# A 2-layer hybrid decoder trunk on one core: weight splits of 128x2048 in one instruction per engine

## The chip, the cores and the metric

One Trainium2 chip, one core. The time is the device time of one execution in microseconds (us), as the median of the runs of a kernel. The engines are TensorE (PE), VectorE (DVE), ScalarE (ACT), GpSimd (POOL) and SyncE (SP); each works through its own queue of instructions in order. TensorE's weight loads are shown apart, as PEld.

## What is computed

256 tokens of 1024 channels pass through two layers in float32. Each layer runs three mixers side by side, merges them with sigmoid gates, projects, and then applies a feed-forward part, which is dense in layer 0 and routed over 8 experts in layer 1.

```python
for l in range(DEPTH):                                   # 2 layers
    z = rms_norm(x, norm_mix_g[l]) @ w_in[l]
    a_x, a_y, m_u, m_o, m_i, m_f, xa_q, gate_pre = split_columns(z)
    xa_c = causal_dwconv(a_x, conv_rg_w[l], conv_rg_b[l])          # 4 taps
    y_rg = rg_lru(xa_c, rg_w_a[l], ..., rg_w_x[l], ...) * gelu(a_y)  # block-diagonal w_a, w_x, then a scan
    y_ml = mlstm_branch(m_u, m_o, m_i, m_f, ...)                   # conv, silu, block-diagonal w_q, w_k, w_v
    y_xa = memory_attention(xa_q, rms_norm(mem, mem_norm_g[l]), w_kv[l])   # 4 heads, softmax over 256 tokens
    x = x + (g0 * (y_rg @ w_br_rg[l]) + g1 * (y_ml @ w_br_ml[l]) + g2 * (y_xa @ w_br_xa[l])) @ w_out[l]
    h2 = rms_norm(x, norm_ffn_g[l])
    x = x + (swiglu(h2, w1, w3, w2) if l == 0 else moe_swiglu(h2, ...))   # 8 experts, 2 per token, inner size 3584
return rms_norm(x, final_norm_g)
```

## The kernel before

Every matmul keeps float32 accuracy by splitting both operands into a rounded part and a remainder. A weight raw becomes whi, a copy rounded to fp32r by ACT (line 115), and wlo = raw - whi, which DVE writes (line 116); both lines are the helper `split`. PE then makes three passes: whi with the rounded activations, whi with their remainder, wlo with the rounded ones (`passes`, line 103).

Weights come from memory as half slabs of 128x2048 (8 KB per partition) into tiles named raw (or rawu, in the expert stage), loaded by SP. `wsplit` splits each half slab in two pieces of 128x1024, each into a pair (whi, wlo) of tiles from a pool with PARTS = 5 buffers for each of the two names. A buffer is free again when PE has read the split that is in it, so a new split can start when the fifth one before it is used up. Where each piece is read depends on the stage:

- `ws_half` and `ws_slab`: weights are stationary, 256 tokens stream. A half slab feeds 48 matmuls of 256 columns. The slabs of the input projections, of the merges and of the output projection (lin.0, lin.1, ...) go this way.
- `wm_slab`: activations are stationary and 512 weight columns stream. linm.0 to linm.3 in layer 0 (linm.8 to linm.11 in layer 1) make the mLSTM's o gate this way, as two slabs; o (line 575) is the sigmoid of a finished bank, mm.
- `rglru` (the recurrence) and `mlstm`: five block-diagonal weights (w_a, w_x, w_q, w_k, w_v), one half slab each, with four blocks or heads. Two blocks were split at a time.
- The dense feed-forward part (`second` in `ffn`) and the expert stage: `wm` for w1 and w3, `second` for w2. In the expert stage there are 8 experts with 7 chunks of 512 inner columns, 56 chunks in all. A chunk reads six half slabs: two of r1, two of r3, two of w2. silu (line 876) needs the whole r1 result, the mul (line 879) needs r3, then PE transposes the product (con,t) and ACT and DVE split it (gh, gl), to be used with the w2 of the chunk in the following one.

Around the places that the change touches: in the attention each head has kT,q matmuls, a row maximum (line 260), exp (line 266), a normalisation (line 270), four transposes (ax<-con,t), a copy of the transposed tile (line 276) and the t,v matmuls; the o gate's matmuls of linm are placed among the heads. In the recurrence the output of lin.8 to lin.11 (mm) is copied by ACT (line 250), scaled by line 285 and gathered by DVE with three taps a block (line 288, conv); gh and gl are the split of the conv's result, which the block-diagonal matmuls read.

The order of instructions on an engine isn't written out in the kernel. The framework takes the program, its dependencies and the buffer pools, and orders each engine's queue; a change of sizes or of buffer numbers moves instructions in all queues.

## Time and profile before

| what | value |
|---|---|
| median of 3 runs | 2062.35 us (2060.28 to 2065.11) |
| profiled execution | 2060.13 us, span 2058.2 us |
| PE, PEld, DVE, ACT, POOL busy | 98%, 87%, 76%, 66%, 0% |
| mean granted TensorE clock | 0.994 |
| splits, raw and rawu | 772 and 228 of 128x1024 |

The stages follow one another: layer 0 until about 630 us, layer 1's mixers from there, the router from 1033 us, the experts from 1049 us to the end. An engine that is busy 98% of the span still has gaps, and what ended each one is read in the timeline, where a row's bracket gives the idle time before it and the instruction that ended it.

### The profile page before, as it was taken

How to read it: one execution, taken by the hardware profiler on the slowest of the kernel's cores; microseconds unless marked ns; L12 is line 12 of the kernel's file. 1: busy time of each engine (PE TensorE's matmuls, PEld its weight loads, DVE VectorE, ACT ScalarE, POOL GpSimd, SP SyncE). 2: the span in 40 equal slices, each digit the busy share in tenths (PEclk: the TensorE clock that was granted, in tenths of full speed). 3: DMA queues.
4: the chain of work that ended last, by engine and by line, in shares of the span. 5: the costliest groups of instructions: out<-in, count | busy, mean ns of one | idle time of the engine just before them, and what ended most of it. 6: DMA issues, size and time to landing. Idle time of an engine off the chain costs nothing.

```text
span 2058.2 us, 31849 instructions
## 1 busy us (share of the span) xinstructions
PE 2014.7 (98%) x12782; PEld 1797.8 (87%) x12782; DVE 1564.9 (76%) x1872; ACT 1352.5 (66%) x1684; POOL 3.9 (0%) x8
## 2 busy tenths in 40 slices
PE   8999999999999999999989999999999999999998
PEld 7989999999999989999968888888787787878886
DVE  8465976665555665965579999988888888888887
ACT  5575954554445566954477877777676777767775
POOL 0000000000000000000000000000000000000000
PEclk9999999999999999999999999999999999999999
DMA  8523365545555523455758898999889998999993
GB/s 328 185 83 123 144 246 193 192 172 201 187 202 186 183 105 103 164 210 205 279 223 320 339 354 352 367 356 350 342 341 350 356 364 342 339 349 353 351 365 128
DMA packets 74315, 531.82 MB, mean 258 GB/s; under 512 B 8624, under 2 KB 8752, under 8 KB 10032
## 3 DMA queue, kind: packets, MB, share of 16 engines
q1 hardware_dynamic: 73296, 528.56, 68.7%
q8 instruction: 102, 1.67, 0.3%
q10 hardware_dynamic: 864, 1.15, 0.2%
q14 instruction: 53, 0.43, 0.1%
HBM read 528.63 MB, written 1.05 MB: 257 GB/s over the span
## 4 chain that ended last, share of the span: by engine, by line
PE 92%; ACT 3%; DVE 3%; issue 1%; DMA 0%; SPq 0%; ACTq 0%; DVEq 0%
PE mm L103 65%; PE ax L103 25%; DVE wlo L116 1%; PE mm L107 1%; ACT whi L115 1%; DVE xc L288 1%; PE ax L107 1%; ACT cv L285 0%; DMA mem<-memT 0%; ACT t L266 0%; ACT u L815 0%; ACT cv L414 0%; DVE y L859 0%; ACT gh L115 0%; ACT L266 0%
## 5 line engine op out<-in xcount | busy, mean ns | idle before, releaser
L116 DVE TENSOR_TENSOR wlo<-raw,whi 128x1024 fp32r<-128x1024 f32 x772 | 925.9, 1221 | 319.9 <-ACT whi L115 313.4
L115 ACT ACTIVATE whi<-raw 128x1024 fp32r<-128x1024 f32 x772 | 800.0, 1059 | 384.9 <-PE mm L103 319.2
L103 PE MATMUL mm<-nh,wlo 128*128 128x256 f32 x1344 | 372.1, 277 | 1.9 <-DVE wlo L116 1.9
L103 PE MATMUL mm<-nh,whi 128*128 128x256 f32 x1344 | 372.2, 277 | 0.0
L103 PE MATMUL mm<-nl,whi 128*128 128x256 f32 x1344 | 371.4, 276 | 0.0
L103 PE MATMUL mm<-wlo,Xh 128*128 128x512 f32 x896 | 354.7, 396 | 4.0 <-DVE wlo L116 3.9
L103 PE MATMUL mm<-whi,Xh 128*128 128x512 f32 x896 | 352.8, 394 | 2.5 <-DVE Xl L775 2.1
L103 PE MATMUL mm<-whi,Xl 128*128 128x512 f32 x896 | 350.0, 391 | 0.0
L116 DVE TENSOR_TENSOR wlo<-rawu,whi 128x1024 fp32r<-128x1024 f32 x228 | 273.4, 1220 | 16.0 <-ACT whi L115 13.3
L103 PEld LDWEIGHTS mm<-nh,wlo 128*128 128x128 f32 x1344 | 252.4, 188 | 2.3 <-DVE wlo L116 2.2
L103 PEld LDWEIGHTS mm<-nl,whi 128*128 128x128 f32 x1344 | 252.4, 188 | 0.1
L103 PEld LDWEIGHTS mm<-nh,whi 128*128 128x128 f32 x1344 | 252.4, 188 | 0.1
L115 ACT ACTIVATE whi<-rawu 128x1024 fp32r<-128x1024 f32 x228 | 230.8, 1054 | 17.1 <-PE mm L103 6.1
L103 PEld LDWEIGHTS mm<-wlo,Xh 128*128 128x128 f32 x896 | 168.3, 188 | 54.6 <-DVE wlo L116 22.1
L103 PEld LDWEIGHTS mm<-whi,Xh 128*128 128x128 f32 x896 | 168.3, 188 | 40.5 <-DVE Xl L775 2.9
L103 PEld LDWEIGHTS mm<-whi,Xl 128*128 128x128 f32 x896 | 168.3, 188 | 33.3
L103 PE MATMUL ax<-wlo,gh 128*128 128x512 f32 (+1 forms) x496 | 191.1, 385 | 0.0
L103 PE MATMUL ax<-whi,gl 128*128 128x512 f32 (+1 forms) x496 | 188.5, 381 | 0.0
L103 PE MATMUL ax<-whi,gh 128*128 128x512 f32 (+1 forms) x496 | 171.9, 379 | 0.0
L103 PEld LDWEIGHTS ax<-whi,gh 128*128 128x128 f32 x496 | 93.1, 188 | 18.2
L103 PEld LDWEIGHTS ax<-wlo,gh 128*128 128x128 f32 x496 | 93.2, 188 | 17.0
L103 PEld LDWEIGHTS ax<-whi,gl 128*128 128x128 f32 x496 | 93.1, 188 | 16.3
(330 smaller groups left out, 2833.2 us busy)
## 6 DMA issues: line engine op xcount, KB each, us to landing
raw<-e SPq DMA_DIRECT2D x222, 1024.0 KB, 6.3
rawu<-e SPq DMA_DIRECT2D x114, 1024.0 KB, 8.3
raw<-lin SPq DMA_DIRECT2D x96, 1024.0 KB, 4.8
raw<-f SPq DMA_DIRECT2D x42, 1024.0 KB, 4.8
raw<-linm SPq DMA_DIRECT2D x16, 1024.0 KB, 4.8
raw<-bdw SPq DMA_DIRECT2D x10, 1024.0 KB, 4.8
mem<-memT SPq DMA_DIRECT2D x4, 512.0 KB, 6.3
x<-xT SPq DMA_DIRECT2D x1, 1024.0 KB, 12.4
```

The source lines that it names most:

```text
L103: nc.tensor.matmul(o, lhsT, rhs, start=start, stop=stop, **kw)
L107: nc.tensor.transpose(o, i, con[0:n, C_ID:C_ID + n])
L115: act(hi, src, AF.Copy)
L116: dve.tensor_sub(lo, src, hi.bitcast(F32))
L288: stt(dst[:, b, s:], src[:, b, :T - s], lcol(l, wo + 8 * k, b), dst[:, b, s:], op0=OP.mult, op1=OP.add)
```

## The change

A half slab is split by one instruction on ACT and one on DVE, and PE's loops read it in the same order of channels as before. The pool has three pairs of 128x2048 instead of five of 128x1024. The block-diagonal weights are split whole, before their loop over heads; the gate weights' pair (gh, gl in line 556) uses the same larger tiles. The scratch memory of the DMA goes from 2048 to 1024.

```diff
-PARTS = 5
+PARTS = 3
...
-    def half(shape, tag, at):
-        return view(wp.tile([P, 1024 + PAD], F32R, tag=tag, name=nm(tag), bufs=PARTS), shape, at)
-
-    def wsplit(src, at):
-        shape = list(src.shape)
-        hi, lo = half(shape, "whi", at[0]), half(shape, "wlo", at[1])
-        split(hi, lo, src)
+    def part(shape, tag, at):
+        return view(wp.tile([P, 2048 + PAD], F32R, tag=tag, name=nm(tag), bufs=PARTS), shape, at)
+
+    def wsplit(raw, at):
+        shape = list(raw.shape)
+        hi, lo = part(shape, "whi", at[0]), part(shape, "wlo", at[1])
+        split(hi, lo, raw)
         return hi, lo
...
     def ws_half(raw, xh, xl, ps):
+        wh, wl = wsplit(raw, WS_AT)
         for h in range(2):
-            wh, wl = wsplit(raw[:, h * 4:(h + 1) * 4], WS_AT)
...
     def wm_slab(src, xh, xl, done):
...
-        for q in range(4):
-            wh, wl = wsplit(raw[q // 2][:, (q % 2) * 2:(q % 2 + 1) * 2], WM_AT)
-            for t in range(2):
-                for k in range(2):
-                    kk = q * 2 + k
+        for q in range(2):
+            wh, wl = wsplit(raw[q], WM_AT)
+            for t in range(2):
+                for k in range(4):
+                    kk = q * 4 + k
...
         raws = (bd_load(0, l), bd_load(1, l))
+        ws_ = [wsplit(w, WS_AT) for w in raws]
         for gg in range(0, 4, 2):
-            ws_ = [wsplit(w[:, gg:gg + 2], WS_AT) for w in raws]
...
+        wv = wsplit(raw, WS_AT)
         for gg in range(0, 4, 2):
-            wv = wsplit(raw[:, gg:gg + 2], WS_AT)
...
         def wm(raw, xh, xl, cs, ps):
-            for q in range(4):
-                wh, wl = wsplit(raw[q // 2][:, (q % 2) * 2:(q % 2 + 1) * 2], WM_AT)
-                for k in range(2):
-                    kk = q * 2 + k
+            for q in range(2):
+                wh, wl = wsplit(raw[q], WM_AT)
+                for k in range(4):
+                    kk = q * 4 + k
...
-    nc = bacc.Bacc("TRN2", target_bir_lowering=False, num_devices=1, dynamic_dma_scratch_size=2048)
+    nc = bacc.Bacc("TRN2", target_bir_lowering=False, num_devices=1, dynamic_dma_scratch_size=1024)
```

The functions `second` of both feed-forward parts and the w_q and w_k loop of `mlstm` are changed in the same way. In what follows a number after a name tells tiles of one name apart; lines of the changed kernel after 620 stand two to four further down than before.

First, ACT at the end of layer 0's attention, before. The exp of head 3 is the second row; mm184 and mm185 are the two banks of the o gate that linm.2 and linm.3 fill:

```order
L266 ACT_TABLE_LOAD
L266 ACTIVATE t2163_1202,asm164_1203<-ax160_1193,anb162_1200 128x256 x2
L414 ACT_TABLE_LOAD
L414 ACTIVATE cv215_1431<-cv215_1431 128x512 x2
L276 ACTIVATE t2167_1215<-ax166_1210 128x512
L115 ACTIVATE whi221_1475<-raw219_1471 128x1024
L414 ACTIVATE cv215_1431<-cv215_1431 128x512
L115 ACTIVATE whi223_1479<-raw220_1473 128x1024
L115 ACTIVATE xah131_1098<-ax168_1217 128x512
L575 ACT_TABLE_LOAD
L575 ACTIVATE o169_1224<-mm184_1301 128x512
L575 ACTIVATE o169_1224<-mm185_1302 128x512
```

The same place in the changed kernel, where these two banks are mm148 and mm149, exp of head 3 is the L266 row with ax128, and whi205 is the split of w_v:

```order
L575 ACT_TABLE_LOAD
L575 ACTIVATE o137_1160<-mm148_1229 128x512
L115 ACTIVATE gh_186_1404<-cv175_1351 128x512
L575 ACTIVATE o137_1160<-mm149_1230 128x512
L115 ACTIVATE gh_190_1442<-cv175_1351 128x512
L266 ACT_TABLE_LOAD
L266 ACTIVATE t2131_1138,asm132_1139<-ax128_1129,anb130_1136 128x256 x2
L115 ACTIVATE whi205_1562<-raw204_1560 128x2048
L276 ACTIVATE t2135_1151<-ax134_1146 128x512
L115 ACTIVATE xah99_1034<-ax136_1153 128x512
```

The exp has moved from ahead of both o copies to behind them, and the split of w_v stands between it and the copy of the transposed tile (L276). On PE the last rows of linm.3, the transposes of head 3 and its t,v matmuls now follow each other:

```order
L103 MATMUL mm149_1230<-whi152_1259,nh23_258 128x512
L103 MATMUL mm149_1230<-wlo153_1260,nh23_258 128x512
L103 MATMUL mm149_1230<-whi152_1259,nl24_259 128x512
L107 MATMUL ax134_1146<-con_74,t2131_1138 128x128 x4
L103 MATMUL ax136_1153<-t2135_1151,v9_122 128x256 x4
```

The last matmul of linm.3 and the transposes that read t2131, which is normalised from that exp, are neighbours; before, five rows of linm.3 stood behind the transposes and seven behind t,v.

Second, DVE at the start of layer 0's recurrence, before. xc is the conv's result, gl_345 and gl_349 are those of blocks 0 and 1, and the L288 rows come in sixes, one six for each bank that lin.8 to lin.11 fill:

```order
L116 TENSOR_TENSOR wlo341_2238<-raw338_2233,whi340_2237 128x1024
L116 TENSOR_TENSOR wlo343_2242<-raw339_2235,whi342_2241 128x1024
L116 TENSOR_TENSOR gl_345_2246<-xc335_2198,gh_344_2245 128x512
L288 SCALAR_TENSOR_TENSOR xc335_2198<-ax304_1932,vec_73,xc335_2198 128x255 x2
L288 SCALAR_TENSOR_TENSOR xc335_2198<-ax304_1932,vec_73,xc335_2198 128x254 x2
L288 SCALAR_TENSOR_TENSOR xc335_2198<-ax304_1932,vec_73,xc335_2198 128x253 x2
L116 TENSOR_TENSOR gl_349_2281<-xc335_2198,gh_348_2280 128x512
L116 TENSOR_TENSOR wlo353_2316<-raw338_2233,whi352_2315 128x1024
L116 TENSOR_TENSOR wlo355_2320<-raw339_2235,whi354_2319 128x1024
L288 SCALAR_TENSOR_TENSOR xc335_2198<-ax304_1932,vec_73,xc335_2198 128x255 x2
```

The same in the changed kernel, where they are gl_291 and gl_295 and the last three L288 rows belong to lin.11's bank, mm272:

```order
L288 SCALAR_TENSOR_TENSOR xc281_2090<-ax258_1840,vec_73,xc281_2090 128x253 x2
L116 TENSOR_TENSOR wlo289_2134<-raw285_2127,whi288_2133 128x2048
L288 SCALAR_TENSOR_TENSOR xc281_2090<-ax258_1840,vec_73,xc281_2090 128x255 x2
L288 SCALAR_TENSOR_TENSOR xc281_2090<-ax258_1840,vec_73,xc281_2090 128x254 x2
L288 SCALAR_TENSOR_TENSOR xc281_2090<-ax258_1840,vec_73,xc281_2090 128x253 x2
L116 TENSOR_TENSOR gl_291_2138<-xc281_2090,gh_290_2137 128x512
L116 TENSOR_TENSOR gl_295_2173<-xc281_2090,gh_294_2172 128x512
L116 TENSOR_TENSOR wlo312_2304<-raw308_2298,whi311_2303 128x2048
```

And ACT there, in the changed kernel (whi311 is the split of lin.12):

```order
L115 ACTIVATE gh_290_2137<-xc281_2090 128x512
L115 ACTIVATE gh_294_2172<-xc281_2090 128x512
L115 ACTIVATE whi311_2303<-raw308_2298 128x2048
L250 ACTIVATE ax258_1840<-mm272_2011 128x512
L285 ACTIVATE xc281_2090<-ax258_1840,vec_73 128x256 x2
```

Both gl have moved behind the last six conv steps, and these need L250's copy of mm272, which stands behind whi311. Before, gl_345 and gl_349 stood ahead of them.

Third, ACT in a late chunk of the experts, before: raw2718 and rawu2719 are r1, raw2720 and raw2721 are r3.

```order
L115 ACTIVATE gh_2716_16543<-mm2715_16538 128x512
L115 ACTIVATE whi2723_16556<-raw2718_16547 128x1024
L115 ACTIVATE whi2725_16566<-raw2718_16547 128x1024
L115 ACTIVATE whi2727_16576<-rawu2719_16549 128x1024
L115 ACTIVATE whi2729_16586<-rawu2719_16549 128x1024
L115 ACTIVATE whi2733_16599<-raw2720_16551 128x1024
L115 ACTIVATE whi2735_16609<-raw2720_16551 128x1024
L876 ACTIVATE t22731_16596<-mm2722_16555 128x512
L115 ACTIVATE whi2737_16619<-raw2721_16553 128x1024
L115 ACTIVATE whi2739_16629<-raw2721_16553 128x1024
L115 ACTIVATE whi2743_16644<-rawu2741_16640 128x1024
```

In the changed kernel, where raw1998 and rawu1999 are r1, raw2000 and raw2001 are r3:

```order
L115 ACTIVATE whi2003_15116<-raw1998_15107 128x2048
L115 ACTIVATE gh_1996_15103<-mm1995_15098 128x512
L115 ACTIVATE whi2005_15132<-rawu1999_15109 128x2048
L115 ACTIVATE whi2009_15151<-raw2000_15111 128x2048
L115 ACTIVATE whi2011_15167<-raw2001_15113 128x2048
L880 ACTIVATE t22007_15148<-mm2002_15115 128x512
L115 ACTIVATE whi2015_15188<-rawu2013_15184 128x2048
L115 ACTIVATE whi2017_15204<-raw2014_15186 128x2048
L115 ACTIVATE whi2027_15238<-raw2022_15229 128x2048
L115 ACTIVATE gh_2020_15225<-mm2019_15220 128x512
```

silu (L876, now L880) has moved from between the two half slabs of r3 to behind both.

## Rows read from the trace of the kernel before

**Rows 1.** The page's busy times: us, share of the span, instructions.
```profile
PE 2014.7 (98%) x12782; PEld 1797.8 (87%) x12782; DVE 1564.9 (76%) x1872; ACT 1352.5 (66%) x1684; POOL 3.9 (0%) x8
```
**Rows 2.** The page's chain that ended last, by engine.
```profile
PE 92%; ACT 3%; DVE 3%; issue 1%; DMA 0%; SPq 0%; ACTq 0%; DVEq 0%
```
**Rows 3.** The page's groups: count | busy us, mean ns | idle before, releaser.
```profile
L116 DVE TENSOR_TENSOR wlo<-raw,whi 128x1024 fp32r<-128x1024 f32 x772 | 925.9, 1221 | 319.9 <-ACT whi L115 313.4
L115 ACT ACTIVATE whi<-raw 128x1024 fp32r<-128x1024 f32 x772 | 800.0, 1059 | 384.9 <-PE mm L103 319.2
```
**Rows 4.** Timeline, late expert chunks, ACT and DVE: start, us, [idle before <-releaser].
```profile
1454.33 2.00 ACT L115 ACTIVATE whi<-raw 128x1024 fp32r<-128x1024 f32 x2
...
1470.99 0.60 ACT L876 ACTIVATE t<-mm 128x512 f32<-128x512 f32 x1 [2.89 <-PE mm L103]
...
1488.12 0.60 ACT L876 ACTIVATE t<-mm 128x512 f32<-128x512 f32 x1 [2.91 <-PE mm L103]
...
1455.41 2.36 DVE L116 TENSOR_TENSOR wlo<-raw,whi 128x1024 fp32r<-128x1024 f32 x2 [1.32 <-ACT whi L115]
```
**Rows 5.** Timeline, early expert chunks, ACT: silu of two neighbouring chunks.
```profile
1119.91 0.60 ACT L876 ACTIVATE t<-mm 128x512 f32<-128x512 f32 x1 [0.30 <-PE mm L103]
...
1136.70 0.60 ACT L876 ACTIVATE t<-mm 128x512 f32<-128x512 f32 x1 [0.30 <-PE mm L103]
```
**Rows 6.** Waits (us in total, times, longest), and one such wait in PE's timeline.
```profile
PEld mm L103 <- DVE wlo L116: 24.7, 63, 1.4
...
1577.41 0.50 PE L103 MATMUL mm<-wlo,Xh 128*128 128x512 f32 x1 [0.93 <-DVE wlo L116]
```
**Rows 7.** Timeline of the start, DVE and PE.
```profile
12.92 1.22 DVE L116 TENSOR_TENSOR wlo<-raw,whi 128x1024 fp32r<-128x1024 f32 x1
...
14.20 0.58 PE L103 MATMUL mm<-memh,wlo 128*128 128x256 f32 x1
```
**Rows 8.** Timeline, end of layer 0's attention, ACT.
```profile
140.23 0.47 ACT L266 ACTIVATE t<-ax,anb 128x256 f32<-128x256 f32 x1
...
141.27 1.28 ACT L414 ACT_TABLE_LOAD   x1
...
143.62 0.58 ACT L276 ACTIVATE t<-ax 128x512 f32<-128x512 f32 x1
...
148.41 1.08 ACT L575 ACTIVATE o<-mm 128x512 f32<-128x512 f32 x2
```
**Rows 9.** Timeline, end of layer 0's attention, PE.
```profile
142.53 0.73 PE L107 MATMUL ax<-con,t 128*128 128x128 f32 x4
...
144.25 1.99 PE L103 MATMUL ax<-t,v 128*128 128x256 f32 x8
145.90 0.58 PE L103 MATMUL mm<-whi,nl 128*128 128x512 f32 x1
...
150.46 0.19 PE L107 MATMUL ax<-con,zM 4*128 4x4 f32 x1 [1.18 <-DVE zM L393]
```
**Rows 10.** Timeline, start of layer 0's recurrence, ACT, DVE and PE.
```profile
221.59 0.58 ACT L250 ACTIVATE ax<-mm 128x512 f32<-128x512 f32 x1
...
217.80 0.69 DVE L116 TENSOR_TENSOR gl<-xc,gh 128x512 fp32r<-128x512 f32 x1
...
223.64 2.46 DVE L288 SCALAR_TENSOR_TENSOR xc<-ax,vec,xc 128x255 f32<-128x255 f32 x6
...
227.29 0.39 PE L103 MATMUL mm<-nh,wlo 128*128 128x256 f32 x1 [0.92 <-DVE wlo L116]
```
**Rows 11.** Windows (us, engines' busy us, PEclk, DMA, GB/s), and PE's timeline, around the router.
```profile
1036.00:1038.00 2.00, 0.00 (x0) 0.00 (x0) 0.68 (x6) 1.75 (x4) 0.00 (x0) 0.75 1.00 414
1046.00:1048.00 2.00, 2.00 (x14) 2.00 (x14) 0.95 (x3) 0.85 (x3) 0.00 (x0) 0.69 0.00 0
150.00:152.00 2.00, 1.54 (x13) 1.55 (x14) 2.00 (x7) 1.98 (x4) 0.00 (x0) 1.00 0.00 0
...
1041.13 0.58 PE L103 MATMUL mm<-mk,con 128*128 128x16 f32 x2 [6.46 <-DVE mk L713]
...
1061.62 0.66 PE L107 MATMUL mm<-con,t 128*128 128x128 f32 x4 [1.66 <-DVE t L879]
```

More of the change, by code (lines that the diff above doesn't have):

```diff
@@ L418, in mlstm @@
         raws = (bd_load(2, l), bd_load(3, l))
+        wq, wk = [wsplit(w, WS_AT) for w in raws]
         for gg in range(0, 4, 2):
-            wq, wk = [wsplit(w[:, gg:gg + 2], WS_AT) for w in raws]
             pk = bank("ax")
-            for g in range(2):
-                b0 = 2 * (gg + g)
+            for g in range(gg, gg + 2):
+                b0 = 2 * g
                 s2 = pair(cv[:, b0:b0 + 2])
@@ L553, in mixer @@
         nc.scalar.dma_start(gw, gif[l])
-        gh = half((P, KB, P), "whi", WS_AT[0])
-        gl = half((P, KB, P), "wlo", WS_AT[1])
+        gh = part((P, KB, P), "whi", WS_AT[0])
+        gl = part((P, KB, P), "wlo", WS_AT[1])
         nc.gpsimd.memset(gh.bitcast(F32), 0.0)
```

22 lines of the change are left out of this document (13 added, 9 removed).

## Prediction, made before the changed kernel was run

> **What bounds the kernel now.** I read the busy shares first, then the chain, then the waits, and last the timelines at the places that the change touches. TensorE (PE) is busy 98% of the span [rows 1], and the chain that ends last is PE for 92% [rows 2]. So a part of the change costs or gives time only where PE waits, and the sum is a list of PE's gaps: those that are there, and those that the new order makes. A split is a pair: ScalarE (ACT) copies raw to whi, VectorE (DVE) writes wlo, and PE needs both. One of 1024 columns takes 1.06 us on ACT and 1.22 us on DVE [rows 3]. PE's weight loads wait for wlo 24.7 us in all [rows 6]; that is all that faster splitting can give back.
>
> **One instruction instead of two.** Two 1024 splits in a row occupy ACT for 2.00 us and DVE for 2.36 us [rows 4], that is one of [rows 3] and 0.94 or 1.14 us more. Part of this second share is the start of an instruction, which the whole split has once, so I estimate 1.9 us for a whole split on ACT (1.8 to 2.0) and 2.3 us on DVE (2.2 to 2.4). The 500 whole splits save ACT some 50 us and DVE 0 to 30 us of busy time, all beside PE. What PE sees is the latency from raw to wlo: 1.06 + 1.22 = 2.3 us before, 4.2 us now.
>
> The Trainium skill ("Perfetto Trace Analysis", Optimizing Scalar/DVE Operations) says that larger operations help where the engine is saturated, and that breaking instructions up may finish work sooner where ACT or DVE is not saturated but leaves bubbles on others. Its figure of some 60 ns for a DVE instruction would make an estimate of 30 us of DVE time; with DVE off the chain the sum stays as it is, and the second half of the rule speaks against this change.
>
> **The start.** The first wlo runs from 12.92 us, and the first matmul that reads it starts at 14.20 us [rows 7]. The whole split takes ACT 0.85 us and DVE 1.1 us longer: **+1.9 us** (1.7 to 2.2). Every later stage begins behind it.
>
> **Attention heads, in each of two layers.** The new order moves head 3's softmax. Before, its exp (L266) is queued ahead of the last two o copies and starts at 140.23; the transposes at 142.53 find PE still busy with linm.3 [rows 8, 9]. Now exp stands on ACT behind the o copy from mm149, which needs the last matmul of linm.3, and the next row of PE after that matmul is the transposes that need this exp. PE has nothing in between. First, ACT comes late itself: from the previous head's pT copy on it has that copy, three silu or xah, two whole splits, a table load, an o copy and a gh, 8.3 us at 0.5, 1.9 and 1.28 us [rows 8]; PE has meanwhile two groups of 1.65 us [rows 9] and 15 matmuls of 0.23 us (16.8 us over a chunk's 72 matmuls, [rows 5]), 7.3 us with the copy that they wait for. That is 1.0 us. Then o 0.54, gh 0.5, table load 1.28, and from exp to the first transpose 2.30 us in the old rows, less a conv step of about 0.6 that lay between, 1.7. Together 5.0 us. Behind exp the whole split of w_v (1.9 us) is queued ahead of the copy that t,v needs: 1.2 us more. Head 1 waits 0.6 us, since its row maximum now stands behind a wlo of 2.3 us, and heads 0 and 2 some 0.4 us. **+7.2 us a layer** (5 to 9).
>
> After them, in w_v's heads, lin.8's whi of 1.9 us stands ahead of the next gh, its wlo of 2.3 us ahead of the next gl, and lin.9's whi ahead of the first mv copy. PE has some 1 us less cover than these take: **+1.0 a layer** (0 to 2).
>
> **The start of the recurrence, in each layer.** Before, gl of block 0 (217.80) precedes the conv of the last two blocks (six L288 in 2.46 us from 223.64), so that two blocks of w_a and w_x matmuls cover that conv; the one gap is 0.92 us [rows 10]. Now gl of blocks 0 and 1 stands on DVE behind these six. And on ACT the whi of lin.12, third split after lin.11's with three pairs of buffers, waits until PE has read lin.11 to its end, with the L250 copy of lin.11's own output queued behind it. From that end: hand-over 0.2, whi 1.9, L250 0.5 [rows 10], about as much for the first L285, six L288 2.46, gl 0.69: 6.3 us, in which PE has 0.7 us of other matmuls. The gap is 5.7 us instead of 0.92: **+4.8 a layer** (3.9 to 5.5).
>
> **The clock.** In the router's gap of 6.46 us the granted clock fell to half (0.75 over 1036 to 1038, when PE had been idle for 2 us), from 2.4 to 1.2 GHz, and it was not quite back in 1046 to 1048 (0.69), 6 us after matmuls resumed at 1041.13 [rows 11]. Some 4 us of PE's work ran at half speed, 2 us lost. Each layer now gets two gaps of 4 to 5 us. I take 2 us for each: **+8** (0 to 9).
>
> The Trainium skill ("TensorE: Matmul & The Clock Gate", Part 1) says that the slow level is the default and activity releases it. The rows agree (0.75 in the gap, 0.69 at its end); by the rule the term is +8, and were it not to hold here, 0.
>
> **Router and first chunk.** The sum of squares now stands behind a wlo, but ACT's table load covers all but 0.3 us. The wait of 1.66 us before the first chunk's transposes [rows 11] shrinks to about 1.0, since DVE then has only the mul, and no longer a wlo, between the last r3 matmul and them. **-0.4** (-1 to +1).
>
> **The experts (MoE).** Early chunks repeat every 16.8 us [rows 5], late ones every 17.13 us [rows 4], with the same matmuls. In the late ones silu waits 2.9 us for PE, and the second r3 splits stand behind it on ACT, so that they come just in time or late. Now silu stands behind both half slabs of r3. Followed by hand with 1.9 and 2.3 us a split, none of a late chunk is late; the closest is the one behind gh, by 0.35 us. Some 30 ordinary late chunks at 0.3 us are 9 us, and five stalls like the one of 0.93 us [rows 6] bring 4. In three chunks that gather tokens the next split stands behind eight Xl and comes 0.7 us late, +2. **-11** (-22 to 0).
>
> **Sum.** 1.9 + 2 x (7.2 + 1.0 + 4.8) + 8 - 0.4 - 11 = +24.5 us on an execution of 2060.13 us (span 2058.2 and 1.9 around it): 2084.6. The median of the runs is 2.2 us above that execution: **2087 us**. The smaller DMA scratch makes room and no more, as the page lists hardware queues alone: 0. The bytes and the queues of the loads stay.
>
> **The rivals.**
> A, faster: the experts give back all 24.7 us of [rows 6], the new stalls are at their low ends (head 3 with ACT not late 4.0 + 0.9, recurrence 3.9, so 17.6 for two layers) and the clock holds: 2062.35 - 24.7 + 17.6 + 1.5 = 2057. It decides the sign if the new stalls stay under some 19 us. For it: every late chunk does lose 0.33 us, and DVE goes from split to split there with 1.32 us of idle time in a chunk's half [rows 4], so it is near its limit. Against it: the stalls come from what stands ahead in the queues, in both layers. Chance 0.08. (By the first half of the skill's rule above, DVE near its limit is the case where larger instructions pay.)
> B, three pairs are too few: the split behind gh has 0.35 us to spare. If a whole split takes 0.2 us longer on each engine, that is gone and the late chunks stay at 17.13; beyond that every 0.1 us costs 3.6 us over 36 chunks. 2087 + 13 = 2100, up to 2107. Chance 0.15.
> C, the clock holds: after the gap of 1.18 us at 150.46 [rows 9] it was 1.00 [rows 11], and the new gaps are broken by short bursts of matmuls. 2087 - 8 = 2079. Chance 0.20.
> D, the new gaps are half covered: PE takes other matmuls there than I read, or ACT is not held by the pair of lin.11. 13 us less and no clock loss: 2066, about no change. Chance 0.09.
>
> **How the numbers follow.** My forecast has the remaining 0.48, from 2080 to 2093. The range leaves out A, D and the upper end of B, 2 in 10 together: 2068 to 2103. Faster by more than 0.2% (4.1 us, about what a measurement can tell from no change here) is A, 0.08; within it is most of D, 0.08; the rest is slower, 0.84.
>
> **What would show it.** In the trace of the changed kernel: in both layers a gap of 4 to 6 us on PE before head 3's transposes, ended by DVE's t; a gap near 4 us before the second matmul of the recurrence's block 0, ended by DVE's gl, with one near 1.7 us just before it, ended by ACT's whi; a granted clock under 1 in these stretches; silu rows 16.9 us apart late in the experts; whi near 1.9 us and wlo near 2.3 us. The prediction is wrong if PE shows no gap at head 3, if wlo exceeds 2.5 us, or if late chunks stay at 17.13 us.

## The result and the profile after

The changed kernel takes **2089.72 us** (median; 2089.19 to 2089.92) beside 2063.73 us for the kernel before on the same chip: a ratio of 1.0128, 95% interval 1.0115 to 1.0141. It is slower by 26 us; forecast were 2087 us in a range of 2068 to 2103. The profiled execution took 2089.64 us, with a span of 2087.9 us against 2058.2 us before. All differences of places below are between two such executions. Their own clock can differ (last section); the medians, taken over several executions, differ by 26.0 us where these two differ by 29.5.

The page of the changed kernel, first TensorE's and the other engines' busy time, then the chain by engine, then the two groups of whole splits:

```profile
PE 2022.7 (97%) x12782; PEld 1816.1 (87%) x12782; DVE 1521.6 (73%) x1372; ACT 1297.5 (62%) x1184; POOL 3.9 (0%) x8
...
PE 89%; ACT 6%; DVE 4%; issue 1%; DMA 0%; SPq 0%; ACTq 0%; DVEq 0%
...
L116 DVE TENSOR_TENSOR wlo<-raw,whi 128x2048 fp32r<-128x2048 f32 x386 | 880.5, 2289 | 278.9 <-ACT whi L115 277.7
L115 ACT ACTIVATE whi<-raw 128x2048 fp32r<-128x2048 f32 x386 | 741.7, 1923 | 472.1 <-PE mm L103 322.6
```

A whole split takes 1.92 us on ACT and 2.29 us on DVE, where one of 1024 columns took 1.06 and 1.22 us [rows 3]. Both engines have less to do and PE has the same matmuls, yet the chain that ended last has gone from PE for 92% [rows 2] to PE for 89%, with 10% on ACT and DVE: PE now waits where it did not.

Where the time went is read from the start of the same row of PE in both traces:

| row of PE | before, us | after, us | later by, us |
|---|---|---|---|
| first matmul that reads a wlo | 14.20 | 16.34 | 2.1 |
| scores of head 0, layer 0 | 108.98 | 111.77 | 2.8 |
| transposes of zM, behind head 3 | 150.46 | 160.51 | 10.1 |
| merge of layer 0 (first xah matmul) | 259.82 | 279.22 | 19.4 |
| transposes of zM, layer 1 | 774.51 | 801.75 | 27.2 |
| merge of layer 1 | 880.67 | 920.77 | 40.1 |
| router | 1041.13 | 1082.93 | 41.8 |
| transposes of the first expert chunk | 1061.62 | 1102.60 | 41.0 |
| transposes of the last expert chunk | 2034.99 | 2065.79 | 30.8 |

The stages ahead of the router lose 41.8 us, and the experts give back 10.2; behind the last chunk's transposes another 1.1 us is won, so that the spans differ by 29.7 us. The timeline of PE in the changed kernel, only the rows of head 3's end (the first five) and of the recurrence's start in layer 0; the number in brackets is PE's idle time before the row:

```profile
152.28 1.10 PE L107 MATMUL ax<-con,t 128*128 128x128 f32 x4 [4.33 <-DVE t L270]
154.06 3.78 PE L103 MATMUL ax<-t,v 128*128 128x256 f32 x8 [0.69 <-ACT t L276]
158.53 0.59 PE L107 MATMUL ax<-con,za 128*4 128x128 f32 x2 [0.46 <-DVE za L384]
...
160.51 0.23 PE L107 MATMUL ax<-con,zM 4*128 4x4 f32 x1 [1.17 <-DVE zM L393]
...
233.81 0.38 PE L103 MATMUL mm<-nh,whi 128*128 128x256 f32 x1 [1.30 <-ACT whi L115]
...
238.88 0.58 PE L103 MATMUL ax<-gl,whi 128*128 128x256 f32 x1 [4.57 <-DVE gl L116]
```

The waits of 4.33 and 4.57 us were not there before: head 3's transposes followed without a gap [rows 9], and the recurrence had one gap of 0.92 us [rows 10]. Layer 1 shows the same (4.32, 0.89, 0.46, 1.18, 1.30 and 4.57 us). The second row shows more than a wait: the eight t,v matmuls take 3.78 us, where they take 1.99 us at the full clock (below, e_head3). The windows of the changed kernel around head 3 (columns: sum, busy time of PE, PEld, DVE, ACT, POOL, then the granted clock as a share of 2.4 GHz, the DMA share, GB/s):

```profile
146.00:150.00 4.00, 1.95 (x9) 1.28 (x7) 4.00 (x5) 3.97 (x6) 0.00 (x0) 1.00 0.83 270
152.00:160.00 8.00, 5.91 (x17) 3.98 (x17) 4.41 (x8) 2.61 (x3) 0.00 (x0) 0.54 0.50 184
160.00:168.00 8.00, 7.49 (x39) 7.02 (x40) 1.25 (x6) 2.63 (x6) 0.00 (x0) 0.61 0.00 0
```

Until 150 us, while PE runs dry, ACT and DVE are busy all the time (3.97 and 4.00 of 4 us), which points to their queues as what PE waits for (e_exp and e_head3 below put this to the test). The clock then stays at or near its lower level of 1.2 GHz until after 166 us, with PE busy for 7.49 of the last 8 us, and is back at 1.00 over 170 to 174 us. Behind the recurrence's gap it is low too: 0.53 over 234 to 245 us, with PE busy for 6.4 us of them.

In the experts, the timeline of ACT in the changed kernel, its silu rows (L880):

```profile
1656.12 0.60 ACT L880 ACTIVATE t<-mm 128x512 f32<-128x512 f32 x1 [0.80 <-PE mm L103]
...
1672.93 0.60 ACT L880 ACTIVATE t<-mm 128x512 f32<-128x512 f32 x1 [0.80 <-PE mm L103]
```

They stand 16.8 us apart, as early chunks do [rows 5], and silu waits 0.80 us for PE instead of 2.9 us [rows 4].

### The profile page after: what moved, and what is told of

Read it like the earlier page. It is cut to its first block, busy times and chain, and to the rows that moved or that the text cites. A ratio compares the mean times of both kernels' runs of the same rounds, so it can differ in the third digit from the quotient of the medians.

```text
span 2087.9 us, 30300 instructions
## 1 busy us (share of the span) xinstructions
PE 2022.7 (97%) x12782; PEld 1816.1 (87%) x12782; DVE 1521.6 (73%) x1372; ACT 1297.5 (62%) x1184; POOL 3.9 (0%) x8
## 4 chain that ended last, share of the span: by engine, by line
PE 89%; ACT 6%; DVE 4%; issue 1%; DMA 0%; SPq 0%; ACTq 0%; DVEq 0%
PE mm L103 63%; PE ax L103 24%; ACT whi L115 2%; DVE wlo L116 1%; PE mm L107 1%; DVE xc L288 1%; PE ax L107 0%; ACT cv L285 0%; DMA mem<-memT 0%; ACT t L266 0%; ACT mlh L525 0%; ACT L266 0%; ACT L575 0%; ACT L414 0%; ACT cv L414 0%
## 5 line engine op out<-in xcount | busy, mean ns | idle before, releaser
L116 DVE TENSOR_TENSOR wlo<-raw,whi 128x2048 fp32r<-128x2048 f32 x386 | 880.5, 2289 | 278.9 <-ACT whi L115 277.7
L115 ACT ACTIVATE whi<-raw 128x2048 fp32r<-128x2048 f32 x386 | 741.7, 1923 | 472.1 <-PE mm L103 322.6
L103 PE MATMUL mm<-wlo,Xh 128*128 128x512 f32 x896 | 349.7, 390 | 0.1
L116 DVE TENSOR_TENSOR wlo<-rawu,whi 128x2048 fp32r<-128x2048 f32 x114 | 261.3, 2292 | 61.1 <-ACT whi L115 61.0
L115 ACT ACTIVATE whi<-rawu 128x2048 fp32r<-128x2048 f32 x114 | 218.1, 1913 | 30.6 <-PE ax L103 23.2
L103 PE MATMUL ax<-whi,gh 128*128 128x512 f32 (+1 forms) x496 | 177.8, 380 | 0.3 <-ACT gh L115 0.3
L103 PE MATMUL ax<-gl,whi 128*128 128x256 f32 x352 | 102.3, 291 | 9.1 <-DVE gl L116 9.1
```

What stands on the lines that cost most here:

```text
L103: nc.tensor.matmul(o, lhsT, rhs, start=start, stop=stop, **kw)
L115: act(hi, src, AF.Copy)
L116: dve.tensor_sub(lo, src, hi.bitcast(F32))
```

## The experiments

Twelve kernels stand beside the kernel before and the changed one. "Router" is how much later than in the kernel before PE reaches the router, "experts" the time from the first chunk's transposes to the last's, both from the profiled execution; the medians are of timed runs. They come from several rounds and chips, in which the kernel before took 2062.92 to 2065.54 us beside them; kernels of different rounds are therefore compared by their ratios.

| kernel | median, us | ratio to before (95%) | router, us | experts, us |
|---|---|---|---|---|
| before | 2063.73 | 1 | 0 | 973.4 |
| changed | 2089.72 | 1.0128 (1.0115 to 1.0141) | +41.8 | 963.2 |
| e_exp | 2091.45 | 1.0131 (1.0114 to 1.0148) | +41.3 | 963.2 |
| e_rec | 2088.63 | 1.0116 (1.0099 to 1.0133) | +36.9 | 966.5 |
| e_both | 2089.13 | 1.0115 (1.0099 to 1.0132) | +37.6 | 966.4 |
| e_head3 | 2085.46 | 1.0103 (1.0086 to 1.0120) | +33.7 | 966.4 |
| k_warm | 2084.46 | 1.0102 (1.0085 to 1.0119) | +35.0 | 963.2 |
| t_all | 2091.28 | 1.0137 (1.0121 to 1.0154) | +31.3 | 972.8 |
| t_mix | 2080.86 | 1.0077 (1.0059 to 1.0094) | +29.2 | 966.6 |
| t_lazy | 2073.58 | 1.0057 (1.0040 to 1.0074) | +24.3 | 963.2 |
| t_order | 2065.33 | 1.0011 (1.0000 to 1.0021) | +18.0 | 963.2 |
| b_hoist | 2070.63 | 1.0039 (1.0024 to 1.0053) | +10.0 | 973.2 |
| b_silu | 2055.06 | 0.9947 (0.9931 to 0.9964) | +5.6 | 964.9 |
| b_silu6 | 2055.79 | 0.9967 (0.9952 to 0.9981) | +4.2 | 964.3 |

### Undoing one queue order at a time: e_exp, e_rec, e_both, e_head3

**e_exp** moves the o copies of the second o-gate slab behind head 3's exp on ACT, since the prediction put the gap on them, and the split of w_v behind its pT copy.

```diff
+                with tc.issue_after(ex.ins):
+                    act(o[:, t, s * 512:(s + 1) * 512], ps, AF.Sigmoid)
...
-        wv = wsplit(raw, WS_AT)
+        with tc.issue_after(pc.ins):
+            wv = wsplit(raw, WS_AT)
```

`tc.issue_after(x)` queues what is issued under it behind x on its engine; ex is head 3's exp, pc its pT copy.

> The changed kernel, with two instructions of ScalarE put elsewhere in its queue at head 3, in each layer: the two o copies of the second o-gate slab go behind head 3's exp instead of ahead of it, and the split of w_v goes behind head 3's pT copy. Split sizes and buffers stay. Theory (the queue orders make the gap, and the gap makes the clock fall): the gap of 4.33 us before head 3's transposes goes to under 1 us, the copy wait of 0.7 us behind it too, and the stretch of low clock that follows it (152 to 166 us, 794 to 808 us) is gone: 4 to 5 us and 4 to 5 us a layer, 16 to 20 us less than the changed kernel, some 2072 us. Rival 1 (the latency of exp, max and normalisation is too long for the PE work that is left, whatever stands in the queue): the gap stays over 2.5 us and the time falls by less than 6 us. Rival 2 (the clock falls for another cause than the gap): the gap goes but the low stretch stays, 8 to 10 us less, some 2080 us.

The gap went from 4.33 to 3.97 us, and the time did not fall. These are rival 1's numbers, but not its reason: what stands in a queue does matter, only DVE's queue is a second limit, right behind ACT's. The timelines of PE, ACT and DVE in e_exp:

```profile
153.42 1.16 PE L107 MATMUL ax<-con,t 128*128 128x128 f32 x4 [3.97 <-DVE t L270]
...
150.46 1.28 ACT L266 ACT_TABLE_LOAD   x1 [2.03 <-DVE anb L262]
...
144.61 2.29 DVE L116 TENSOR_TENSOR wlo<-raw,whi 128x2048 fp32r<-128x2048 f32 x1 [1.76 <-ACT whi L115]
146.82 0.68 DVE L116 TENSOR_TENSOR xal<-ax,xah 128x512 fp32r<-128x512 f32 x1
147.42 0.68 DVE L260 TENSOR_REDUCE amx<-ax 128x2 f32<-128x512 f32 x1
148.02 2.28 DVE L116 TENSOR_TENSOR wlo<-raw,whi 128x2048 fp32r<-128x2048 f32 x1
150.22 0.16 DVE L262 TENSOR_SCALAR anb<-amx 128x2 f32<-128x2 f32 x1
```

These two wlo are w_q's and w_k's. The row maximum amx waits behind the first, its scaled copy anb behind the second, and exp needs anb. On ACT, freed from the o copies, the table load ahead of exp sat idle for 2.03 us until anb was there.

**e_rec** gives the recurrence the order of the kernel before: conv and pairs block by block, and lin.12's and lin.13's splits behind the last conv scale.

```diff
-        conv(xc, ax, l, V_RGW, V_RGB)
...
+                last = conv(xc, ax, l, V_RGW, V_RGB, range(b0, b0 + 2))
                 s2 = pair(xc[:, b0:b0 + 2])
...
+        with tc.issue_after(last.ins):
+            for s in range(2):
+                ws_slab(lin[l, S_AY + s], ...)
```

> The changed kernel, with the start of the recurrence ordered as in the kernel before: conv blocks and the pairs of w_a and w_x follow one another block by block in the program, so that gl of block 0 stands on VectorE ahead of the conv of the last blocks; and the splits of lin.12 and lin.13 go behind the last conv scale on ScalarE, so that they no longer stand ahead of the copy of lin.11's output. Split sizes and buffers stay. Theory: the gaps of 1.30 and 4.57 us at 234 to 239 us and 875 to 880 us shrink to 1 us together, and the low clock of 234 to 245 us and 876 to 887 us goes: 5 us and 3 us a layer, 14 to 17 us less than the changed kernel, some 2074 us. Rival 1 (three pairs are too few: the splits of lin.12 and lin.13, now later, are late for their matmuls): the gap moves behind the recurrence, to the first matmul of lin.12, as 2 to 4 us, and half of the gain or less is left, some 2082 us. Rival 2 (the gap is the conv's own latency): both gaps stay over 3 us together, 2086 us or more.

The timeline and a window of PE in e_rec:

```profile
233.31 0.50 PE L103 MATMUL ax<-gh,whi 128*128 128x256 f32 x2 [1.34 <-ACT gh L115]
...
240.12 1.02 PE L103 MATMUL ax<-gh,whi 128*128 128x256 f32 x4 [1.45 <-ACT gh L115]
...
236.00:238.00 2.00, 2.00 (x11) 2.00 (x11) 2.00 (x6) 1.97 (x3) 0.00 (x0) 0.50 0.00 0
```

The two gaps of 1.30 and 4.57 us became 1.34, 0.23 and 1.45 us, 2.9 us less a layer where the theory had 4.9 less. So the order makes more than half of the new wait there, and 3.0 us are left, which is where rival 2 begins. The clock fell all the same (0.50 over 236 to 238 and 242 to 244 us), so the router came 4.9 us earlier and not 14. Of this 3.2 us went again in the experts (966.5 instead of 963.2 us), where the clock fell behind two gaps that are in both kernels (last section). In the timed runs the ratio is 1.0116 beside 1.0128, no clear difference.

**e_both** has both edits.

> The changed kernel with both edits, at head 3 and at the recurrence; split sizes and buffers stay. Theory (the loss outside the experts is queue order, not the size of the instructions): the gains of the two edits add up, 30 to 36 us less than the changed kernel, 2054 to 2060 us, which is at or below the kernel before, since the experts' 11 us and the later start of 2.6 us are left. Rival (a larger instruction delays everything behind it, and what is taken away at two places comes back at others): less than 20 us of it, over 2070 us.

The rival's number came (2089.13 us, ratio 1.0115): two edits that win next to nothing each win next to nothing together.

**e_head3** frees both queues at head 3: w_q's splits behind its exp, w_k's behind its pT copy, the o copies behind these, w_v's behind the exp of zem.

```diff
+        with tc.issue_after(ex.ins):
+            wq = wsplit(raws[0], WS_AT)
+        with tc.issue_after(pc.ins):
+            wk = wsplit(raws[1], WS_AT)
+        with tc.issue_after(last_hi[0].ins):
+            for t, ps in late:
+                act(o[:, t, 512:1024], ps, AF.Sigmoid)
```

> The changed kernel with head 3's softmax freed on both engines, in each layer: the splits of w_q go behind head 3's exp, those of w_k behind its pT copy, the two o copies of the second o-gate slab behind these, and the split of w_v behind the exp of zem. (In e_exp, where ScalarE's o copies alone were moved, VectorE still had two whole wlo ahead of the row maximum and its scaled copy anb, and the gap was 3.97 us.) Theory (the queues of both engines make the gap, each whole wlo by 2.3 us): the row maximum comes some 2.5 us earlier, anb some 4.8 us, and the gap before head 3's transposes falls from 4.33 us to under 1.5 us with the copy wait under 0.5 us; with the clock up again, 6 to 9 us a layer, 12 to 18 us less than the changed kernel, 2072 to 2078 us. Rival 1 (the clock falls anyway): 3 to 4 us a layer, 2082 us. Rival 2 (the work put off is late at its next user): the gaps before za and zM, 0.46 and 1.17 us, grow by what was won, and the time stays within 4 us of 2089 us.

The list late holds the banks of the second o-gate slab, and last_hi is the whi of w_k. The timeline of PE in e_head3:

```profile
148.60 0.81 PE L107 MATMUL ax<-con,t 128*128 128x128 f32 x4 [0.53 <-DVE t L272]
150.30 1.99 PE L103 MATMUL ax<-t,v 128*128 128x256 f32 x8 [0.89 <-ACT t L278]
155.29 0.38 PE L107 MATMUL ax<-con,za 128*4 128x128 f32 x2 [2.88 <-DVE za L387]
...
156.96 0.23 PE L107 MATMUL ax<-con,zM 4*128 4x4 f32 x1 [1.18 <-DVE zM L396]
```

The gap fell to 0.53 us, and t,v ran at full clock. But the wait for za grew from 0.46 to 2.88 us, since the splits that were put off now stand ahead of it on DVE (two whole wlo from 149.79 to 154.37 us): the four gaps sum to 5.5 us instead of 6.7. Behind that wait the clock was low all the same, with PE busy throughout:

```profile
158.00:166.00 8.00, 8.00 (x35) 7.28 (x35) 1.23 (x3) 3.61 (x5) 0.00 (x0) 0.50 0.11 44
```

The router came 8.1 us earlier, 3.2 us of that was lost to the clock in the experts, and 4.3 us are left in the median: theory in the gap, rival 2 in the time.

### What the idle time alone costs: k_warm

16 matmuls are added between linm.3's last matmul and head 3's transposes.

```diff
+        spare = bank()
+        with tc.issue_after(last_mm[0].ins):
+            for i in range(16):
+                mm(spare, hh[:, 0, 0:P], hh[:, 0:2].rearrange("p b t -> p (b t)"), True, True)
```

> The changed kernel with 16 matmuls of 128x512 more in each layer, on operands that are there, into a spare PSUM bank that nothing reads; they stand on TensorE between the last matmul of linm.3 and head 3's transposes, where it waits 4.33 us, and take some 3.7 us. No wait is taken away: this asks what the idleness alone costs. Theory (the idle gap makes the clock fall): the granted clock stays at 1.00 from 152 to 166 us and from 794 to 808 us, some 5 us a layer, 8 to 10 us less than the changed kernel, 2080 us. Rival (the clock falls there for what follows, short matmuls and transposes, and not for the gap): the low stretch stays, and the time stays at 2089 us.

The windows of k_warm:

```profile
152.00:158.00 6.00, 3.42 (x17) 2.44 (x17) 4.44 (x8) 2.44 (x3) 0.00 (x0) 1.00 0.33 104
158.00:164.00 6.00, 5.70 (x32) 5.32 (x33) 1.04 (x6) 1.87 (x5) 0.00 (x0) 0.72 0.30 128
```

Adding work to PE made the kernel **faster by some 5 us** (2084.46 against 2089.72, ratio 1.0102 against 1.0128; the router 6.8 us earlier). No dependence was shortened; the transposes start at 152.21 us as in the changed kernel (152.28), but the clock is 1.00 over 152 to 158 where it was 0.54 over 152 to 160. So the idle gap does cause the long fall there. The gain is about half of what was expected, since a shorter fall comes later (0.72 over 158 to 164).

### Length of the instructions, or the large pairs: t_all, t_mix

**t_all** keeps the three large pairs and splits each half slab by two instructions of 1024 columns per engine.

```diff
-        split(hi, lo, raw)
...
+            n = shape[1] // 2
+            for h in range(2):
+                c = slice(h * n, (h + 1) * n)
+                split(hi[:, c], lo[:, c], raw[:, c])
```

> The changed kernel with its three pairs of large buffers and its smaller scratch, but each half slab split by two instructions of 1024 columns per engine, everywhere. Theory (the length of the instructions and the order that follows from it make the loss, and the experts' gain too): the stages before the experts as in the kernel before, at head 3 and at the recurrence no gap over 1.3 us, late expert chunks 17.1 us apart, 2060 to 2068 us in all. Rival (the three large pairs, fewer buffers in turn, make the loss): 2080 us or more.

The rival held. The start of 2.1 us is gone and the gap at the recurrence is smaller, but head 3 still has 2.56, 1.00, 2.07 and 1.64 us, and the router is 31.3 us late. The timeline of PE in t_all:

```profile
148.42 0.81 PE L107 MATMUL ax<-con,t 128*128 128x128 f32 x4 [2.56 <-DVE t L276]
150.22 3.64 PE L103 MATMUL ax<-t,v 128*128 128x256 f32 x8 [1.00 <-ACT t L282]
156.10 0.38 PE L107 MATMUL ax<-con,za 128*4 128x128 f32 x2 [2.07 <-DVE za L390]
...
158.23 0.24 PE L107 MATMUL ax<-con,zM 4*128 4x4 f32 x1 [1.64 <-DVE zM L399]
...
233.90 0.58 PE L103 MATMUL ax<-gl,whi 128*128 128x256 f32 x1 [2.67 <-DVE gl L116]
```

So of the 41.8 us some 10 belong to the instructions' length, with the order that follows from it, and some 31 to the rest of the change. In the experts, where silu again stands ahead of the last splits of r3, nothing is gained (972.8 us).

**t_mix** is t_all with whole splits in the experts alone.

> As t_all, but in the experts half slabs are split whole, as in the changed kernel: one instruction per engine there, two elsewhere. Theory (loss outside the experts, gain inside, and they are independent): the router is reached as in t_all, the experts take 11 to 12 us less than in the kernel before, 2050 to 2056 us in all, which would beat both kernels. Rival (the gain in the experts needs what comes before them): over 2060 us.

The experts won as expected, 10.4 us in the median against t_all; the 2050 to 2056 us missed because t_all had not come back to 2063.

### The large pairs or the move ahead of the loops: b_hoist, t_lazy, t_order

The block-diagonal weights (w_q and w_k, w_v, w_a and w_x) are split whole ahead of their loops in the changed kernel. **b_hoist** does this alone to the kernel before.

```diff
+        wa = [[wsplit(w[:, gg:gg + 2], WS_AT) for gg in (0, 2)] for w in raws]
         for gg in range(0, 4, 2):
-            wq, wk = [wsplit(w[:, gg:gg + 2], WS_AT) for w in raws]
+            wq, wk = [w[gg // 2] for w in wa]
```

> The kernel before, with five pairs of 1024 columns, in which only one thing of the change is done: the block-diagonal weights (w_q and w_k, w_v, w_a and w_x) are split ahead of their loops, both halves, instead of half by half inside. t_all showed that three large pairs with two instructions per half slab lose 31 us ahead of the router; it has this move and the large pairs. Theory 1 (the move loses it: twice the split work must be done before the first head of w_q can start): the router is reached 15 to 31 us later than in the kernel before, 2078 to 2094 us in all. Theory 2 (the large pairs lose it, since a pair is taken and given back as a whole): the router at most 5 us later, 2062 to 2069 us in all.

The router came 10.0 us later (7.7 us in the medians), between the two theories: the move by itself costs at most a third of what t_all lost. Head 3's transposes had no gap; PE waited 1.87 us for zrw (an exp on ACT behind w_k's whi) and 0.58 and 0.95 us at the recurrence.

**t_lazy** is t_mix with the second halves split inside the loops again.

```diff
-        wq, wk = [wsplit(w, WS_AT) for w in raws]
+        wq, wk = [lazy(w) for w in raws]
         for gg in range(0, 4, 2):
+            lazy_half((wq, wk), raws, gg)
```

> As t_mix (three large pairs; whole splits in the experts, two instructions per half slab elsewhere), but of the block-diagonal weights only the first half is split ahead, and the second where the kernel before splits it, into the second half of the same pair. Theory 1 (the move makes the loss ahead of the router): the router is reached 5 to 14 us later than in the kernel before instead of 29 us, 2055 to 2066 us in all. Theory 2 (the large pairs make it): the router 22 to 30 us later, 2073 to 2081 us in all.

Here `lazy` takes a pair and splits nothing, and `lazy_half` splits 1024 columns into it. The recurrence's gaps fell to 0.58, 0.50 and 0.96 us, head 3's stayed (2.67, 1.00, 2.07, 1.33 us), and the router is 24.3 us late: theory 2's number, at its lower end in the time. What was left to explain is why head 3 waits although no instruction is long and no more is split ahead than before. The timeline of ACT in t_mix, which has the same order there (L272 is an exp, in the first row head 1's and in the last head 2's; L282 is head 1's pT copy, L291 the conv of the mLSTM):

```profile
121.23 0.46 ACT L272 ACTIVATE t<-ax,anb 128x256 f32<-128x256 f32 x1
...
124.99 0.59 ACT L282 ACTIVATE t<-ax 128x512 f32<-128x512 f32 x1
125.47 2.56 ACT L291 ACTIVATE cv<-mu,vec 128x256 f32<-128x256 f32 x5
...
133.72 0.47 ACT L272 ACTIVATE t<-ax,anb 128x256 f32<-128x256 f32 x1
```

The conv stands between heads 1 and 2, and head 2's exp comes 12.5 us after head 1's. In the kernel before, these exps (the first two rows) are 8.4 us apart, and the conv begins behind head 2's pT copy, which starts at 131.49:

```profile
120.27 0.47 ACT L266 ACTIVATE t<-ax,anb 128x256 f32<-128x256 f32 x1 [2.12 <-DVE anb L262]
...
128.68 0.46 ACT L266 ACTIVATE t<-ax,anb 128x256 f32<-128x256 f32 x1
...
132.46 2.07 ACT L285 ACTIVATE cv<-mu,vec 128x256 f32<-128x256 f32 x4
```

PE does not wait at head 2: it takes o-gate matmuls in the meantime. But those are what covered head 3, and between head 3's scores and its transposes 14 are left in PE's queue instead of 30 (the expectation below counts one more in each case). The changed kernel has the same order, with its conv from 128.91 us and 15 matmuls left. **t_order** puts ACT's order at the heads back in t_lazy: the conv, the halves of w_q and w_k and the o copies of the second slab, and nothing else.

```diff
-        conv(cv, u, l, V_MLW, V_MLB)
+        with tc.issue_after(pc2.ins):
+            conv(cv, u, l, V_MLW, V_MLB)
...
+            with tc.issue_after((ex if gg == 0 else pc).ins):
+                lazy_half((wq, wk), raws, gg)
+            if gg == 0:
+                with tc.issue_after(last_hi[0].ins):
+                    for t, ps in late:
+                        act(o[:, t, 512:1024], ps, AF.Sigmoid)
```

> As t_lazy (three large pairs; whole splits in the experts alone; the block-diagonal weights split by halves), and in the attention of each layer ScalarE's queue is put back to the order of the kernel before: the conv of the mLSTM behind head 2's pT copy instead of between heads 1 and 2, the first halves of w_q and w_k behind head 3's exp, the o copies of the second o-gate slab behind these, the second halves behind head 3's pT copy. TensorE's queue then has 28 matmuls of linm.3 between head 3's scores and its transposes instead of 15 (31 in the kernel before). Large pairs and their number stay. Theory (with large pairs later work enters the queues ahead of the heads' softmax, and it is this order that costs, not the pairs): the gaps of 2.7, 1.0, 2.1 and 1.3 us at head 3 shrink to some 2.5 us together, the low clock behind them goes, 6 to 8 us a layer, 2058 to 2062 us in all. Rival (a pair that comes free late holds the splits up, whatever the order): the gaps move behind head 3, to w_q's heads, and the time stays over 2069 us.

In the edit pc2 is head 2's pT copy. The timeline of PE in t_order, and two windows behind head 3, of layer 0 and of layer 1:

```profile
145.56 0.81 PE L107 MATMUL ax<-con,t 128*128 128x128 f32 x4
147.38 1.99 PE L103 MATMUL ax<-t,v 128*128 128x256 f32 x8 [1.00 <-ACT t L291]
149.95 0.38 PE L107 MATMUL ax<-con,za 128*4 128x128 f32 x2 [0.46 <-DVE za L403]
...
152.68 0.19 PE L107 MATMUL ax<-con,zM 4*128 4x4 f32 x1 [2.24 <-DVE zM L412]
...
152.00:158.00 6.00, 4.91 (x24) 4.39 (x25) 2.33 (x9) 3.98 (x9) 0.00 (x0) 0.72 0.00 0
...
782.00:792.00 10.00, 9.47 (x42) 8.92 (x43) 3.90 (x10) 6.81 (x12) 0.00 (x0) 0.50 0.07 10
```

Head 3's transposes have no gap, t,v runs in 1.99 us, and the four gaps sum to 3.7 us instead of 7.1. The median is 8.3 us lower, 2065.33 us, and the ratio to before went from 1.0057 to 1.0011 (1.0000 to 1.0021). Pairs and splits are those of t_lazy, so it is the order that takes head 3's gap away. The theory came out in part: the zM wait grew from 1.33 to 2.24 us, the low clock behind head 3 (0.52 over 148 to 162 in t_lazy) became short in layer 0 but not in layer 1, and the time is 3 to 7 us above the forecast. In the profile the router came 6.3 us earlier, nearly all of it idle time, and is still 18.0 us late. Which of the three moved pieces does it was not separated.

### The experts by themselves: b_silu, b_silu6

**b_silu** is the kernel before with the silu of a chunk put behind the splits of r3, where the changed kernel has it.

```diff
-                act(s1, p1, AF.Silu)
                 p3 = bank()
                 wm(r3, xh, xl, cs, p3)
+                with tc.issue_after(last_hi[0].ins):
+                    act(s1, p1, AF.Silu)
```

> The kernel before with one instruction moved: in each expert chunk the silu goes on ScalarE behind the splits of r3, where the changed kernel has it, instead of ahead of the last of them. Splits of 1024 columns, buffers and everything else stay. Theory (the experts' gain comes from this order, not from larger instructions): late chunks repeat every 16.8 us instead of 17.15 us, the wait of 24.7 us for wlo falls by half or more, and the time falls by 8 to 14 us, some 2052 us. Rival (the gain comes from fewer, larger instructions and their buffers): late chunks stay at 17.1 us and the time within 3 us of 2063 us.

The theory held but for one number: 10.5 us less than the kernel before on the same chip, ratio 0.9947 (0.9931 to 0.9964), the fastest kernel here. The timeline of ACT in b_silu, silu rows (L881) of two late chunks:

```profile
1620.15 0.60 ACT L881 ACTIVATE t<-mm 128x512 f32<-128x512 f32 x1 [0.30 <-PE mm L103]
...
1637.02 0.60 ACT L881 ACTIVATE t<-mm 128x512 f32<-128x512 f32 x1 [0.30 <-PE mm L103]
```

16.87 us apart instead of 17.13, and the experts take 964.9 us, 8.5 of the 10.2 us that the changed kernel wins there. The wait of PE's weight loads for wlo fell from 24.7 us [rows 6] to 16.5 us only, a third and not half. So most of the gain is the order's; the larger instructions and pairs add some 2 us.

**b_silu6** adds a sixth small pair, in the room that the smaller scratch leaves (each tile is 64 columns shorter for it).

> As b_silu (the kernel before with silu behind the splits of r3), with six pairs of 1024 columns instead of five, which need the smaller scratch; that is the room of three pairs of 2048, in small pieces. Theory (room in small pieces does no harm and gives the splits more lead): 2048 to 2055 us; the waits of 0.92 us for wlo that five pairs leave in the experts go, some 5 us, and nothing is lost ahead of the router. Rival (more lead lets splits run ahead of the softmax and delays it, as the large pairs do): the router 10 us or more later, over 2062 us.

2055.79 us, no better than b_silu: the sixth pair wins nothing in the time, four waits of 0.92 us stay in the experts, and the weight loads still wait 13.7 us for wlo in all. But it does no harm ahead of the router either (+4.2 us, beside b_silu's +5.6 without any change there). The rival fell: the same room in small pieces, with the smaller scratch, is harmless.

## Why the prediction was right, and where its working was not

**Sign and size** came out (2089.72 us against 2087). That the sum is so close is luck in part: the two terms of the attention were 7 us too high together and the clock 5 to 9 us too low, and one reason was corrected by the runs.

**What bounds it:** right. The time is PE's gaps, at the places named: head 3, the recurrence, the router, the chunks.

**One instruction instead of two:** 1.92 and 2.29 us, as estimated (1.9 and 2.3). But this step carried too much. The working took the stalls as those of a 2 us instruction in front of a short one; t_all, with no such instruction, still loses 31.3 of the 41.8 us. What delays head 3 is work queued ahead of the heads' softmax: w_q's and w_k's splits (e_head3), and in t_lazy, where no more is split ahead than before, the order that t_order undid. Whether that work is one instruction or two matters little (4.33 us of gap against 2.56, and 2.07 instead of 0.46 at za).

**The start:** 2.1 us at the first wlo, 2.8 by head 0, against 1.9 (1.7 to 2.2). Right, a little low.

**Attention:** +7.2 a layer against 4.7 (4.33 + 0.69 + 0.46 + 1.17, less the 0.80 and 1.18 of before). Mis-sized: the transposes wait 4.3 and not 5.0 us, the copy 0.7 to 0.9 and not 1.2, and no gap is seen at head 1 or in w_v's heads, where another 1.0 a layer was forecast. (ACT's 8.3 us in it add up to 8.1 from the parts named.) And its chain was one-sided. It followed ACT (o copy, table load, exp) to the end; e_exp showed DVE's chain (wlo, amx, wlo, anb) to be only 0.4 us shorter.

**The recurrence:** +4.8 a layer against 4.95 (1.30 + 4.57 - 0.92). Right, at the places and behind the engines named. (6.3 less 0.7 us is 5.6 and not 5.7.) The cause is shown for a part: e_rec, which put gl and the L250 copy ahead again, took 2.9 of the 5.0 us away, and two instructions for one (t_all) leave 0.58 and 2.67 us.

**The clock:** +8, range 0 to 9, against some 17 us in this pair of traces. This is the term that failed. Layer 0 is 16.6 us later from head 0 to the merge, of which 9.8 us are new idle time, so 6.8 are left for the clock; in layer 1 the same stretch is 20.0 us later with 9.9 us of idle time, so 10.1 are left. Of these last, 3 to 4 us come from the one execution of the kernel before and not from the change: b_silu and b_silu6, with about its gaps, lose 3.4 and 4.1 us on that part (last section). Some 13 us remain, still beyond the range. The step was "I take 2 us for each" gap, from the router, where matmuls ran some 4 us at half speed [rows 11]. After head 3's gap they do so for 14 us, some 5 us lost, and after the recurrence's for 6, some 3 us lost (estimates from PE's busy time at 0.5 in the windows above). What keeps the clock low for so long behind head 3 was not tested by itself; the waits of 0.69, 0.46 and 1.17 us follow there. The rule of the Trainium skill ("TensorE: Matmul & The Clock Gate", Part 1), that activity releases the slow level, agrees in direction with k_warm (1.00 over 152 to 158 us with matmuls in the gap, 0.54 over 152 to 160 without); the size is in no row of the kernel before.

**Router and first chunk:** -0.4 against -0.8, of which the wait before the transposes gives 0.34 (1.66 to 1.32 us, and not to 1.0). Not foreseen: 1.37 us in layer 1 ahead of its feed-forward, for mgl, the remainder of the merged channels (DVE).

**The experts:** -11 against -10.2. Right in size, place and cause, and b_silu shows the order alone to give 8.5 us of it. The three gather chunks, forecast at +2, have a gap of 1.3 us each, 3.9 in all.

**The rivals:** C (the clock holds) fell by the windows, D by the gaps. B fell: 16.80 us a late chunk. A's experts came with 10.2 of its 24.7 us, and its small stalls did not. Against the Trainium skill's page ("Perfetto Trace Analysis", Optimizing Scalar/DVE Operations) the trace agrees with the second half, on breaking instructions up: neither engine is saturated over the span (73% and 62%), and PE got the bubbles. But undoing the size alone, as t_all does, takes away only a quarter of the loss.

**What stays open:** t_order is 18.0 us late at the router in its profile. Its new gaps over 0.4 us make some 7 of these, the rest is nearly all clock, and how much of that another execution would give back is not known (b_silu has 5 us of it without a change there). So order is shown as the cause of head 3's gap, of more than half of the recurrence's new wait and of most of the experts' gain, and not of the whole loss. Why the conv comes earlier (the order is computed when the kernel is built) was not followed up: it does so in t_lazy, with large pairs, and in neither b_hoist nor b_silu6. The 10 us between t_all and the changed kernel were not split further than the 2.0 us of the start.

## What to carry to other kernels

Where two helper engines feed the bound one, an edit to buffer sizes is an edit to their queues: look for which softmax, scan or copy now stands behind the work that was pulled forward, and follow both helpers' chains, since freeing one leaves the other (e_exp). Undo the edit's parts one by one before believing the reason that gave the right number: here 8.5 of the experts' 10.2 us came from one moved silu, and without the rest of the change it makes the kernel 10.5 us faster (b_silu). A gap of 4 us on TensorE is to be priced with the slow clock behind it (here another 5 us at head 3), and where nothing else can fill it, matmuls that nobody reads can win a part back (k_warm, some 5 us in two layers).
